# Index scores of a sparse-attention kernel: the low-key passes of two heads in the two halves of the array's rows

## The chip, the core and the metric

The kernel runs on one NeuronCore of a Trainium2 chip. The metric is the time on the device of one execution, in microseconds; lower is better.

## The reference, cut to what matters

The program is one step of a decoder layer: for a prompt of 2048 tokens and for 8 samples it computes a gated DeltaNet group and a sparse attention group from one input projection, then an output projection and a SwiGLU FFN. The change concerns the "lightning indexer" of the prompt's sparse attention, which scores every key for every query before the 256 best keys are chosen:

```python
def _index_scores(iq, ik, iw):
    dots = jnp.einsum('bqhd,bsd->bqhs', iq.astype(jnp.float32), ik.astype(jnp.float32))
    return jnp.einsum('bqh,bqhs->bqs', iw.astype(jnp.float32), jax.nn.relu(dots))
...
    def block(xs):
        q_b, iq_b, iw_b, t0 = xs
        qpos = t0 + jnp.arange(QBLOCK)
        score = _index_scores(iq_b, ik, iw_b)
        score = jnp.where(key_pos[None, None, :] <= qpos[None, :, None], score, -jnp.inf)
        _, idx = lax.top_k(score, topk)
```

There are 8 index heads of dimension 64, one key head for all of them, and blocks of 128 queries (16 blocks). Block i sees (i+1)·128 keys; blocks 0 and 1 need no scores, since they have no more than 256 keys.

## The kernel before, in words

**Split operands.** TensorE multiplies in a rounded format (float32r). So most operands are kept as a high part, rounded to that format, and a low part, the rest; `mm3` (L184 to L186) makes a projection or FFN product of three: high·high, high·low and low·high. These products, 128 × 128 by 512 columns, are the bulk of the work ("FFN products" below, though the input projection uses the same lines). They write PSUM banks tagged "d".

**The index.** A query head has 64 dimensions and the array 128 rows. So `tok` stores, per head, the high part in rows 0 to 63 and the low part in rows 64 to 127 of `iqT_d` (L1040 copies, L1041 subtracts, L1045 transposes), and `narrow` stores keys so that both halves of the rows hold the same high parts (tile a = 0) or the same low parts (a = 1). In `index`, per block and per chunk of up to 512 keys, each head makes two products over all 128 rows into one bank tagged "s" (L1721): (high + low query) with the high keys, then with the low keys. ScalarE applies relu from PSUM (L1723, tile `rl`), and VectorE multiplies by the head's weight and adds to the score row `sc` (L1726, L1728, L1730). There are two "s" banks, used by all of the side work: index, attention scores (L1766), transposes of the norm (L485) and others. `select` then finds the threshold of the 256 best, and `attend` does the attention: scores (L1766), transposed probabilities (L1795, "g" banks), values (L1783).

**Order.** PE runs in an order that a planner writes: `weave` keeps several generators (samples, indices, attends, and the feed, which is projection and FFN) and picks one at each step. A generator yields its PE time, a wait, and the bank that it needs next (`need`) or takes (`use`); `step` books when banks come free from planned times of VectorE and ScalarE. A share (`PACE`) sets when the feed goes ahead of the side work. Where the side work's planned PE time changes, the whole order behind it shifts. DMAs are issued by SP's queue in program order. The FFN of a group of 512 tokens (four groups, `ffn`) begins when the attention of its four blocks is done. Each FFN group has the output projection in 16 steps of 12 products, then a norm whose transposes (L485) need all of it, then the FFN's own steps.

**Other users of a part of the array.** The 32-wide inverse (L1079, L1087, L1092), its 64-wide step (L1122, L1127), the modulation in four strips of 32 columns (L424) and transposes of 8 rows for the samples (L2053) are products that use less than 128 rows or columns.

Of the kernel before, what the change touches and what calls it, by code (L numbers as in the profile page):

```python
# [25 lines left out]
F32 = mybir.dt.float32  # L26
F32R = mybir.dt.float32r
U8 = mybir.dt.uint8
BF = mybir.dt.bfloat16
AF = mybir.ActivationFunctionType  # L30
OP = mybir.AluOpType
# [81 lines left out]
class K:  # L113
# [442 lines left out]
    def weave(self, work, ends):  # L556

        ends = list(ends)
        while ends:
            for w in work:  # L560
                if w["until"] is not None and w["until"]():
                    w["at"], w["until"] = max(w["at"], self.now), None
            able = [(max(w["at"], min(self.free[w["need"]]) if w["need"] else 0), w) for w in work if w["until"] is None]
            self.now = max(self.now, min(t for t, w in able))
            able = [w for t, w in able if t <= self.now]
            w = next((w for w in able if w["early"] and self.spent >= self.share()), able[0])
            if w["early"]:
                with self.tc.high_priority(offset=EARLY):
                    said = next(w["run"], None)
            else:  # L570
                said = next(w["run"], None)
            if said is None:
                work.remove(w)
                if w in ends:
                    ends.remove(w)
            elif callable(said):
                w["until"], w["need"] = said, None
            else:
                self.step(w, *said[:2], **(said[2] if len(said) > 2 else {}))

    def step(self, w, pe, wait, use=None, hold=None, drop=None, need=None, after=False, by=None, **work):

        self.now += pe
        self.spent += 0 if w["early"] else pe
        ends = self.busy(w["early"], **work)
        end = (ends[by] if by else max(ends.values(), default=self.now - LAG)) + LAG
        for tag, at in ((use, end), (hold, GONE_BY)):
            if tag:
                f = self.free[tag]
                f[f.index(min(f))] = at  # L590
        if drop:
            f = self.free[drop]
            f[f.index(GONE_BY)] = end
        w["at"], w["need"] = max(self.now + wait, end if after else 0), need
# [381 lines left out]
    def tok(self, what, blk, a, rows):  # L976
        nc, p, O = self.nc, self.p1, self.O
        R = slice(0, rows)
        tk = slice(blk * 128, blk * 128 + 128)
        samp = blk == 16  # L980

        def P():
            return self.ps.tile([128, 512], F32, name="s", tag="s", bufs=2)

        if what == "aq":
            self.rope(a[R].rearrange("p (h d) -> p h d", h=H), self.ra, blk, rows, H, 16, "ropea")
            yield 0, 3
            pt = P()
            for h in range(H):
                self.o(nc.tensor.transpose(pt[:, h * rows:(h + 1) * rows], a[R, h * 128:(h + 1) * 128], self.id[R, R]))  # L990
            if samp:
                nc.scalar.copy(self.qTs, pt[:, :32].rearrange("p (h n) -> p h n", h=H))
                yield 0.1, 0
                return
            q = self.m("qo")[:, :512]
            nc.scalar.copy(q, pt)
            nc.sync.dma_start(self.qT_d[blk], q)
            yield TP, 0
        elif what == "kv":
            self.rope(a[R, 0:256].rearrange("p (h d) -> p h d", h=2), self.ra, blk, rows, 2, 16, "ropea")  # L1000
            yield 0, 2.5
            pt = P()
            for h in range(2):
                self.o(nc.tensor.transpose(pt[:, h * rows:(h + 1) * rows], a[R, h * 128:(h + 1) * 128], self.id[R, R]))
            pv = pt[:, :2 * rows].rearrange("p (h n) -> p h n", h=2)
            if samp:
                nc.scalar.copy(self.kTs, pv)
                nc.vector.tensor_copy(self.vs[R], a[R, 256:512])
                nc.sync.dma_start(O[7][0, :, 0].rearrange("n h d -> n (h d)"), a[R, 0:256])
                nc.sync.dma_start(O[8][0, :, 0].rearrange("n h d -> n (h d)"), a[R, 256:512])  # L1010
                yield 0.1, 0
                return
            q = self.m("qo")[:, :512]
            nc.scalar.copy(q[:, :256], pt[:, :256])
            nc.sync.dma_start(self.kT_d[:, :, tk].rearrange("h p n -> p h n"), q[:, :256].rearrange("p (h n) -> p h n", h=2))
            nc.sync.dma_start(self.V_d[tk], a[:, 256:512])
            nc.sync.dma_start(O[2][0, 0, tk].rearrange("n h d -> n (h d)"), a[:, 0:256])
            nc.sync.dma_start(O[3][0, 0, tk].rearrange("n h d -> n (h d)"), a[:, 256:512])
            yield TP / 2, 0
        else:  # L1020
            self.rope(a[R].rearrange("p (h d) -> p h d", h=8), self.ri, blk, rows, 8, 8, "ropei")
            if samp:
                yield 0, 3
                pt = P()
                for b in range(2):
                    x = self.m("iqs")[:NS, :512].rearrange("p (h a c) -> p h a c", h=4, a=2)
                    for e in range(2):
                        nc.scalar.copy(x[:, :, e, :], a[R, b * 256:(b + 1) * 256].rearrange("p (h c) -> p h c", h=4))
                    for h in range(4):
                        self.o(nc.tensor.transpose(pt[:, (b * 4 + h) * NS:(b * 4 + h + 1) * NS], x[:, h].rearrange("p a c -> p (a c)"), self.id[R, R]))  # L1030
                for e in range(2):
                    E = slice(e * 64, e * 64 + 64)
                    nc.scalar.copy(self.iqB[E, :, e * 8:e * 8 + 8], pt[E, :64].rearrange("p (h n a) -> p n a h", h=8, a=2)[:, :, e, :])
                yield 0.3, 0
                return

            for b in range(2):
                x = self.m("iqs", F32R)[:, :512].rearrange("p (h a c) -> p h a c", h=4, a=2)
                v = a[:, b * 256:(b + 1) * 256].rearrange("p (h c) -> p h c", h=4)
                nc.scalar.copy(x[:, :, 0, :], v)  # L1040
                nc.vector.tensor_tensor(x[:, :, 1, :], v, x[:, :, 0, :].bitcast(F32), op=OP.subtract)  # L1041
                yield 0, 2 if b else 5
                pt = P()
                for h in range(4):
                    self.o(nc.tensor.transpose(pt[:, h * 128:(h + 1) * 128], x[:, h].bitcast(F32).rearrange("p a c -> p (a c)"), self.id))  # L1045
                q = self.m("qo")[:, :512]
                nc.scalar.copy(q, pt)
                nc.sync.dma_start(self.iqT_d[blk, :, b * 512:(b + 1) * 512], q)
                yield TP, 0
# [657 lines left out]
    def index(self, i, B, general):  # L1707
        nc, p = self.nc, B["pool"]
        n = (i + 1) * 128
        if i >= 2:  # L1710
# [1 line left out]
            iq = B["iqT"]().rearrange("p (h n) -> p h n", h=8)  # L1712
            nc.sync.dma_start(iq, self.iqT_d[i].rearrange("p (h n) -> p h n", h=8))
            sc = B["sc"]()
            yield 0, 5, dict(need="s")
            for c, w in self.widths(n):
                s = sc[:, c * 512:c * 512 + w]
                for h in range(8):
                    ps = self.ps.tile([128, 512], F32, name="s", tag="s", bufs=2)
                    for a in range(2):  # L1720
                        self.o(nc.tensor.matmul(ps[:, :w], iq[:, h, :].bitcast(F32R), B["ikT"][c * 2 + a][:, :w].bitcast(F32R), start=a == 0, stop=a == 1))  # L1721
                    r = B["rl"]()
                    nc.scalar.activation(r[:, :w], ps[:, :w], AF.Relu)  # L1723
                    iw = self.iw[:, i, h:h + 1]
                    if h == 0:
                        nc.vector.tensor_scalar(s, r[:, :w], iw, None, op0=OP.mult)  # L1726
                    elif h == 7 and sums is not None:
                        nc.vector.scalar_tensor_tensor(s, r[:, :w], iw, s, op0=OP.mult, op1=OP.add, accum_out=sums[:, c:c + 1])  # L1728
                    else:
                        nc.vector.scalar_tensor_tensor(s, r[:, :w], iw, s, op0=OP.mult, op1=OP.add)  # L1730
                    yield 2 * MM * w / 512, max(0, self.load["dve"][1] - self.now - 0.8), dict(
                        act=0.16 + 0.44 * w / 512, dve=0.12 + 0.72 * w / 512, by="act", use="s", need="s")
            bias = B["bias"]()
            if general:
                nc.vector.tensor_tensor(sc[:, n - 128:n], sc[:, n - 128:n], self.caus, op=OP.add)
# [432 lines left out]
```

## Time and profile before

| | us |
|---|---|
| median of 3 runs (3600.11 to 3610.41) | 3608.34 |
| the profiled execution | 3607.71 |
| its span, first to last instruction | 3605.8 |
| PE busy in it | 3362.7 (93%) |
| index products, L1721, busy | 170.6 in two groups by tile: 576 and 32 |

Rows of the profile name line, engine, operation, output tile <- input tiles, then rows*columns of the array, the moving operand's shape, and the count. "Busy" of PE and the mean length of one product hold the pipeline's latency (about 0.4 us for a product that starts 0.23 us after the one before it); the time that a product takes from the others is the distance between starts, which the timeline shows. PEld rows are weight loads, which overlap products.

### The profile page before, as it was taken

To read this page: it belongs to the slowest core of one execution; us is meant where nothing else is said; L and a number is where in the kernel's file an instruction comes from. 1 tells how busy PE (TensorE), PEld (TensorE's weight loads), DVE (VectorE), ACT (ScalarE), POOL (GpSimd) and SP (SyncE) were. 2 spreads that over 40 slices of the span, in tenths; PEclk is the share of its full clock that TensorE was granted. 3 is DMA by queue.
4 is the path that set the end of the run, shared out by engine and by line. 5 is a ranking of instruction groups with operands and counts; after the bars stand their busy time and mean duration, and the time that the engine had idled before them with its cause. 6 is when DMAs were issued, how large, how long until landed. Compare 5 with 4: busy or idle time off the path is not lost.

```text
span 3605.8 us, 60166 instructions
## 1 busy us (share of the span) xinstructions
PE 3362.7 (93%) x21994; PEld 2601.9 (72%) x21994; DVE 2122.1 (59%) x4502; ACT 1472.4 (41%) x2855; POOL 593.4 (16%) x539
## 2 busy tenths in 40 slices
PE   8899989989997988999998999999899999899997
PEld 5667767767775767777766777777677777677775
DVE  5555635645743656666767655666766654554545
ACT  4333322422433333444456455454545643332323
POOL 1000001100000113222220121222112112222223
PEclk9999999999998999999999999999999999999999
DMA  8754764665686244455354344335433333522221
GB/s 287 241 185 157 224 232 145 219 221 175 212 274 212 92 143 126 140 165 164 122 200 140 119 148 152 102 105 194 138 95 108 98 102 103 181 76 82 78 83 57
DMA packets 421013, 549.60 MB, mean 152 GB/s; under 512 B 50020, under 2 KB 287817, under 8 KB 420698
## 3 DMA queue, kind: packets, MB, share of 16 engines
q1 hardware_dynamic: 420690, 545.62, 47.7%
q8 instruction: 175, 2.87, 0.3%
q14 instruction: 132, 1.08, 0.1%
q10 hardware_dynamic: 16, 0.03, 0.0%
HBM read 441.78 MB, written 122.70 MB: 157 GB/s over the span
## 4 chain that ended last, share of the span: by engine, by line
PE 53%; DVE 6%; issue 3%; ACT 2%; DMA 2%; SPq 1%; POOL 1%; DVEq 0%; ACTq 0%; POOLq 0%
PE d L184 13%; PE d L186 13%; PE d L185 12%; PE s L1721 3%; PE s L1766 3%; PE g L1783 3%; PE g L1795 1%; DVE wi L168 1%; PE g L200 1%; PE g L201 1%; DMA wr<-in_w_ffn_in_dram 1%; DMA wr<-in_w_out_dram 1%; ACT bias L1590 1%; ACT wi L167 0%; DVE ca L1857 0%
## 5 line engine op out<-in xcount | busy, mean ns | idle before, releaser
L184 PE MATMUL d<-hh,wi 128*128 128x512 f32 x1616 | 694.8, 430 | 26.5 <-DVE tm L1857 6.3
L185 PE MATMUL d<-hl,wi 128*128 128x512 f32 x1616 | 643.8, 398 | 5.3 <-DVE hl L489 5.1
L168 DVE TENSOR_TENSOR wi<-wr,wi 128x512 fp32r<-128x512 f32 x525 | 396.1, 755 | 419.6 <-ACT wi L167 413.9
L186 PE MATMUL d<-hh,wi 128*128 128x512 f32 x1616 | 643.0, 398 | 0.0
L167 ACT CAST wi<-wr 128x512 fp32r<-128x512 f32 x525 | 324.4, 619 | 702.4 <-PE d L186 396.4
L184 PEld LDWEIGHTS d<-hh,wi 128*128 128x128 f32 x1616 | 310.6, 192 | 122.4 <-issue 21.0
L185 PEld LDWEIGHTS d<-hl,wi 128*128 128x128 f32 x1616 | 311.2, 193 | 75.8 <-issue 10.1
L186 PEld LDWEIGHTS d<-hh,wi 128*128 128x128 f32 x1616 | 310.0, 192 | 69.8 <-DVE wi L168 0.4
L184 PE MATMUL d<-wi,hh 128*128 128x512 f32 x736 | 317.3, 431 | 19.1 <-DMA wi<-kept 11.5
L185 PE MATMUL d<-wi,hh 128*128 128x512 f32 x736 | 292.2, 397 | 0.4 <-DVE wi L168 0.4
L186 PE MATMUL d<-wi,hl 128*128 128x512 f32 x736 | 291.7, 396 | 0.3 <-issue 0.3
L184 PE MATMUL d<-wi,ah 128*128 128x512 f32 x616 | 263.4, 428 | 9.2 <-ACT ah L2102 5.4
L2103 POOL TENSOR_TENSOR al<-ca,ah 128x512 fp32r<-128x512 f32 x88 | 121.8, 1394 | 907.0 <-ACT ah L2102 906.8
L186 PE MATMUL d<-wi,al 128*128 128x512 f32 x616 | 245.2, 398 | 2.5 <-POOL al L2103 2.5
L185 PE MATMUL d<-wi,ah 128*128 128x512 f32 x616 | 244.2, 396 | 0.0
L1730 DVE SCALAR_TENSOR_TENSOR sc<-rl,iw,sc 128x512 f32<-128x512 f32 (+3 forms) x224 | 174.9, 781 | 75.0 <-ACT rl L1723 69.0
L1723 ACT ACTIVATE rl<-s 128x512 f32<-128x512 f32 (+3 forms) x288 | 151.4, 543 | 151.7 <-PE s L1721 127.5
L1858 POOL TENSOR_TENSOR xt<-xt,tm 128x512 f32<-128x512 f32 x96 | 141.2, 1482 | 401.3 <-DVE tm L1857 339.3
L184 PEld LDWEIGHTS d<-wi,hh 128*128 128x128 f32 x736 | 140.7, 191 | 64.1 <-DMA wi<-kept 16.2
L1590 ACT ACTIVATE bias<-sc,sv 128x640 bf16<-128x640 f32 (+11 forms) x120 | 169.9, 1416 | 35.7 <-DVE sv L1592 22.9
L1721 PE MATMUL s<-ik,iqT 128*128 128x512 f32 (+3 forms) x576 | 170.6, 392 | 9.2 <-DMA iqT<-iqT_d 4.9
L186 PEld LDWEIGHTS d<-wi,hl 128*128 128x128 f32 x736 | 140.5, 191 | 32.2 <-issue 0.3
(570 smaller groups left out, 5952.8 us busy)
## 6 DMA issues: line engine op xcount, KB each, us to landing
wi<-kept SPq DMA_DIRECT2D x168, 512.0 KB
wr<-in_w_ffn_in_dram SPq DMA_DIRECT2D x584, 128.0 KB
wr<-in_w_ffn_out_dram SPq DMA_DIRECT2D x148, 256.0 KB
kept<-wi SPq DMA_DIRECT2D x56, 512.0 KB
row<-in_w_ada_dram SPq DMA_DIRECT2D x32, 512.0 KB
wr<-in_w_in_dram SPq DMA_DIRECT2D x56, 256.0 KB
xt<-in_x_prompt_dram SPq DMA_DIRECT2D x7, 2048.0 KB
kT<-kT_d SPq DMA_DIRECT2D x54, 256.0 KB
```

What stands on the lines that cost most here:

```text
L167: nc.scalar.copy(hi, wr)
L168: nc.vector.tensor_tensor(lo, wr, hi.bitcast(F32), op=OP.subtract)
L184: self.o(nc.tensor.matmul(out, wh, xh, start=start, stop=False, **kw))
L185: self.o(nc.tensor.matmul(out, wh, xl, start=False, stop=False, **kw))
L186: self.o(nc.tensor.matmul(out, wl, xh, start=False, stop=stop, **kw))
L1590: nc.scalar.activation(c, s, AF.Sign, bias=t, accum_out=cnt)
L1721: self.o(nc.tensor.matmul(ps[:, :w], iq[:, h, :].bitcast(F32R), B["ikT"][c * 2 + a][:, :w].bitcast(F32R), start=a == 0, stop=a == 1))
L1723: nc.scalar.activation(r[:, :w], ps[:, :w], AF.Relu)
L1730: nc.vector.scalar_tensor_tensor(s, r[:, :w], iw, s, op0=OP.mult, op1=OP.add)
L1766: self.o(nc.tensor.matmul(ps[:, :w], qT[:, h, :], kT[:, :w], start=True, stop=True))
L1858: (nc.vector if soon else nc.gpsimd).tensor_tensor(xt, xt, tm, op=OP.add)
L2103: nc.gpsimd.tensor_tensor(al[b], a, ah[b].bitcast(F32), op=OP.subtract)
```

## The change

Heads are taken in pairs. Both heads make their product with the high keys over all 128 rows as before. The product with the low keys uses the high query part alone, over 64 rows: the even head's lies in rows 0 to 63, and odd heads are now stored the other way round, so that theirs lies in rows 64 to 127. The product of the two low parts is left out. The two 64-row products write different "s" banks. A pair now takes two banks at a time, and the planner learns to wait for two; it counts three products for a pair where it counted four.

```diff
-            able = [(max(w["at"], min(self.free[w["need"]]) if w["need"] else 0), w) for w in work if w["until"] is None]
+            able = [(max(w["at"], sorted(self.free[w["need"][0]])[len(w["need"]) - 1] if w["need"] else 0), w) for w in work if w["until"] is None]
...
-        for tag, at in ((use, end), (hold, GONE_BY)):
-            if tag:
+        for tags, at in ((use, end), (hold, GONE_BY)):
+            for tag in tags or ():
...
-                nc.scalar.copy(x[:, :, 0, :], v)
-                nc.vector.tensor_tensor(x[:, :, 1, :], v, x[:, :, 0, :].bitcast(F32), op=OP.subtract)
+                for e in range(2):
+                    nc.scalar.copy(x[:, e::2, e, :], v[:, e::2])
+                    nc.vector.tensor_tensor(x[:, e::2, 1 - e, :], v[:, e::2], x[:, e::2, e, :].bitcast(F32), op=OP.subtract)
...
-            yield 0, 5, dict(need="s")
+            yield 0, 5, dict(need="ss")
...
-                for h in range(8):
-                    ps = self.ps.tile([128, 512], F32, name="s", tag="s", bufs=2)
-                    for a in range(2):
-                        self.o(nc.tensor.matmul(ps[:, :w], iq[:, h, :].bitcast(F32R), B["ikT"][c * 2 + a][:, :w].bitcast(F32R), start=a == 0, stop=a == 1))
-                    r = B["rl"]()
-                    nc.scalar.activation(r[:, :w], ps[:, :w], AF.Relu)
...
-                    yield 2 * MM * w / 512, max(0, self.load["dve"][1] - self.now - 0.8), dict(
-                        act=0.16 + 0.44 * w / 512, dve=0.12 + 0.72 * w / 512, by="act", use="s", need="s")
+                for h2 in range(0, 8, 2):
+                    ps = [self.ps.tile([128, 512], F32, name="s", tag="s", bufs=2) for _ in range(2)]
+                    kh, kl = [B["ikT"][c * 2 + a][:, :w].bitcast(F32R) for a in range(2)]
+                    for e in range(2):
+                        self.o(nc.tensor.matmul(ps[e][:, :w], iq[:, h2 + e, :].bitcast(F32R), kh, start=True, stop=False))
+                    for e in range(2):
+                        half = slice(e * 64, e * 64 + 64)
+                        self.o(nc.tensor.matmul(ps[e][:, :w], iq[half, h2 + e, :].bitcast(F32R), kl[half], start=False, stop=True))
+                    for e in range(2):
+                        h = h2 + e
+                        r = B["rl"]()
+                        nc.scalar.activation(r[:, :w], ps[e][:, :w], AF.Relu)
...
+                    yield 3 * MM * w / 512, max(0, self.load["dve"][1] - self.now - 0.8), dict(
+                        act=0.32 + 0.88 * w / 512, dve=0.24 + 1.44 * w / 512, by="act", use="ss", need="ss")
```

What it does to the order is shown at three places. On PE, the first products of the index in the main loop over blocks (`ik_…` are the tiles of high and low keys, `iqT` the queries, `cf` the identity, `s` and `raws` the samples' convolution rows), before:

```order
L1333 MATMUL g<-cf,raws 8x128 x4
L1721 MATMUL s<-ik_14209,iqT 128x512
L1721 MATMUL s<-ik_14210,iqT 128x512
L184 MATMUL d<-hh,wi 128x512
L185 MATMUL d<-hl,wi 128x512
L186 MATMUL d<-hh,wi 128x512
```

and after:

```order
L1334 MATMUL g<-cf,raws 8x128 x4
L1723 MATMUL s<-ik_14306,iqT 128x512 x2
L1726 MATMUL s<-ik_14307,iqT 128x512 x2
L184 MATMUL d<-hh,wi 128x512
L185 MATMUL d<-hl,wi 128x512
L186 MATMUL d<-hh,wi 128x512
```

One head's two products have become one pair's four, the last two of 64 rows (L1726). Between pairs stand three FFN products or more.

On PE at the norm in the third FFN group (`xt` the rows to transpose, `big` and `PT` the attention's probabilities, `hh`, `hl` the normalised rows), before:

```order
L186 MATMUL d<-wi,hl 128x512
L1795 MATMUL g<-cf,big 128x128 x8
L1783 MATMUL g<-PT,V 128x256 x2
L1795 MATMUL g<-cf,big 128x128 x4
L1783 MATMUL g<-PT,V 128x256 x2
L485 MATMUL s<-cf,xt 128x128 x8
L1795 MATMUL g<-cf,big 128x128 x4
L1783 MATMUL g<-PT,V 128x256 x2
L184 MATMUL d<-hh,wi 128x512
```

and after (L1773 is the line of the attention's scores):

```order
L186 MATMUL d<-wi,hl 128x512
L485 MATMUL s<-cf,xt 128x128 x8
L1773 MATMUL s<-kT,qT 128x512
L184 MATMUL d<-hh,wi 128x512
L185 MATMUL d<-hl,wi 128x512
```

Sixteen transposes and six value products of attention have left this place, and one score product has come. At the same place of the second group 17 products other than the norm's stood before, and 34 now. The last attention block ends 183 FFN products ahead of the fourth group before, and 45 now.

On ScalarE, in a block of the index with a chunk of 512 and one of 384 keys (`rl<-s` are the relus, `PT<-g` the attention's copies, `wi<-wr` the weights' casts), before:

```order
L1723 ACTIVATE rl<-s 128x512 x2
L167 CAST wi<-wr 128x512
L1798 COPY PT<-g 128x512
L1723 ACTIVATE rl<-s 128x512 x2
L1798 COPY PT<-g 128x512
L1723 ACTIVATE rl<-s 128x512 x2
```

and after:

```order
L1730 ACTIVATE rl<-s 128x512 x2
L1805 COPY PT<-g 128x512
L167 CAST wi<-wr 128x512
L1730 ACTIVATE rl<-s 128x512 x2
L1805 COPY PT<-g 128x512 x2
L1730 ACTIVATE rl<-s 128x512 x2
```

The relus come in twos there in both; what stands between two twos has moved by a copy or a cast.

More of the change, by code (lines that the diff above doesn't have):

```diff
@@ L1714, in index @@
             sc = B["sc"]()
-            yield 0, 5, dict(need="s")
+            yield 0, 5, dict(need="ss")
             for c, w in self.widths(n):
                 s = sc[:, c * 512:c * 512 + w]
-                for h in range(8):
-                    ps = self.ps.tile([128, 512], F32, name="s", tag="s", bufs=2)
-                    for a in range(2):
-                        self.o(nc.tensor.matmul(ps[:, :w], iq[:, h, :].bitcast(F32R), B["ikT"][c * 2 + a][:, :w].bitcast(F32R), start=a == 0, stop=a == 1))
-                    r = B["rl"]()
[L1723 to L1730, printed above, removed]
-                    yield 2 * MM * w / 512, max(0, self.load["dve"][1] - self.now - 0.8), dict(
-                        act=0.16 + 0.44 * w / 512, dve=0.12 + 0.72 * w / 512, by="act", use="s", need="s")
@@ new lines, in index @@
+                for h2 in range(0, 8, 2):
[10 more added lines that the diff above has]
+                        nc.scalar.activation(r[:, :w], ps[e][:, :w], AF.Relu)
+                        iw = self.iw[:, i, h:h + 1]
+                        if h == 0:
+                            nc.vector.tensor_scalar(s, r[:, :w], iw, None, op0=OP.mult)
+                        elif h == 7 and sums is not None:
+                            nc.vector.scalar_tensor_tensor(s, r[:, :w], iw, s, op0=OP.mult, op1=OP.add, accum_out=sums[:, c:c + 1])
+                        else:
+                            nc.vector.scalar_tensor_tensor(s, r[:, :w], iw, s, op0=OP.mult, op1=OP.add)
+                    yield 3 * MM * w / 512, max(0, self.load["dve"][1] - self.now - 0.8), dict(
+                        act=0.32 + 0.88 * w / 512, dve=0.24 + 1.44 * w / 512, by="act", use="ss", need="ss")
```

## The prediction

> **What bounds the kernel now.** I read the page's busy shares first, then its chain of work that ended last, then the table of windows for the stretch in which the index runs.
>
> ```profile
> PE 3362.7 (93%) x21994; PEld 2601.9 (72%) x21994; DVE 2122.1 (59%) x4502; ACT 1472.4 (41%) x2855; POOL 593.4 (16%) x539
> ...
> PE 53%; DVE 6%; issue 3%; ACT 2%; DMA 2%; SPq 1%; POOL 1%; DVEq 0%; ACTq 0%; POOLq 0%
> ```
> ```profile
> core 0: us, PE busy (x) PEld busy (x) DVE busy (x) ACT busy (x) POOL busy (x), PEclk, DMA share, GB/s
> 944.00:2853.00 1909.00, 1788.64 (x9810) 1387.39 (x9808) 1202.10 (x2553) 901.45 (x1658) 344.75 (x302) 0.97 0.47 146
> ```
> TensorE is busy 93% of the span and holds most of the chain. In the 1909 us from the first index product to the last it is busy 94% at a granted clock of 0.97; VectorE has 63% and ScalarE 47%. PE runs its instructions in written order, and projection or FFN products stand between nearly all index products. So a microsecond added to or taken from PE there is, but for little, a microsecond of the span.
>
> **What the removed products cost.** The rows by form give the number of index products of each width, two per head, so four per pair of heads.
>
> ```profile
> L1721 PE MATMUL s<-ik,iqT 128*128 128x512 f32 x432 | 140.8, 420 | 8.6 <-DMA iqT<-iqT_d 4.9 <-ACT rl L1723 3.6
> ...
> L1721 PE MATMUL s<-ik,iqT 128*128 128x384 f32 x48 | 12.4, 352 | 0.1
> ...
> L1721 PE MATMUL s<-ik,iqT 128*128 128x256 f32 x48 | 9.0, 289 | 0.5 <-ACT rl L1723 0.5
> ...
> L1721 PE MATMUL s<-ik,iqT 128*128 128x128 f32 x48 | 8.4, 274 | 0.0
> ...
> L1721 PE MATMUL s<-gzc,sq 128*128 128x512 f32 x16 | 4.9, 399 | 0.0
> ...
> L1721 PE MATMUL s<-gzc,sq 128*128 128x384 f32 x16 | 4.2, 352 | 0.9 <-ACT decb L1723 0.9
> ```
> (432+16)/4 = 112 pairs of width 512, (48+16)/4 = 16 of 384, 12 of 256 and 12 of 128: 152 pairs, or 112 + 16·0.75 + 12·0.5 + 12·0.25 = 133 in units of 512 columns. The means (420 ns) hold the pipeline's latency and are no price. The price is the distance between starts, in the timeline of one head among FFN products (start, length, engine and line):
>
> ```profile
> 2818.06 0.39 PE L186 MATMUL d<-hh,wi 128*128 128x512 f32 x1
> 2818.29 0.62 PE L1721 MATMUL s<-ik,iqT 128*128 128x512 f32 x2
> 2818.75 0.39 PE L184 MATMUL d<-hh,wi 128*128 128x512 f32 x1
> ```
> Two products take 2818.75 − 2818.29 = 0.46 us, 0.23 each, and weight loads are hidden. A pair's two second passes are thus 0.46 us at 512 columns; I scale the others by width. If the two halves run side by side they take one stream of 0.23, and the other 0.23 is the gain: 133 × 0.23 = 30.6 us.
>
> **What the new form adds: leaving and re-entering the whole array.** No product of 64 rows and 128 columns is in this trace, so I bound its cost by the products that use a part of the array. The row nearest in shape is the transposes at L2053: 8 rows, all 128 weight columns, alone between FFN products.
>
> ```profile
> 3579.69 0.40 PE L186 MATMUL d<-kT,al 128*128 128x512 f32 x1
> 3580.01 0.28 PE L2053 MATMUL s<-cf,s 8*128 8x8 f32 x2
> 3580.23 0.50 PE L184 MATMUL d<-wi,ah 128*128 128x512 f32 x1
> 3580.56 0.39 PE L185 MATMUL d<-wi,ah 128*128 128x512 f32 x1
> ```
> ```profile
> 3580.01 0.19 PEld L2053 LDWEIGHTS s<-cf,s 8*128 8x128 f32 x2 [0.37 <-issue]
> 3580.22 0.19 PEld L184 LDWEIGHTS d<-wi,ah 128*128 128x128 f32 x1
> 3580.33 0.19 PEld L185 LDWEIGHTS d<-wi,ah 128*128 128x128 f32 x1
> ```
> The start after L186 comes 0.32 later, not 0.23, and the weight load starts only then, after 0.37 us of idling in which nothing is waited for: it isn't pulled ahead. On the way back the load of L184 starts with the product itself, and the product after it comes 0.33 later. From L186 to L185 pass 0.87 us; the two whole products in it are 0.46; so two loads of 128 columns with nearly nothing streamed (8 columns) cost 0.41 us. In the new kernel's pair two loads of 128 columns stand in the same place, with a stream behind them. Two other excursions bound this.
>
> ```profile
> 237.81 0.40 PE L186 MATMUL d<-wi,hl 128*128 128x512 f32 x1
> 238.14 1.14 PE L1122 MATMUL g<-low,NT 64*64 64x64 f32 x16
> 239.21 0.50 PE L184 MATMUL d<-wi,hh 128*128 128x512 f32 x1
> 239.55 0.39 PE L185 MATMUL d<-wi,hh 128*128 128x512 f32 x1
> ```
> ```profile
> 448.81 0.39 PE L186 MATMUL d<-wi,hl 128*128 128x512 f32 x1
> 449.12 1.06 PE L424 MATMUL s<-row,cT 128*32 128x512 f32 x8
> 450.12 0.50 PE L184 MATMUL d<-wi,hh 128*128 128x512 f32 x1
> 450.46 0.39 PE L185 MATMUL d<-wi,hh 128*128 128x512 f32 x1
> ...
> L424 PE MATMUL s<-row,cT x128: 592/617/1062, 449.1 to 1150.5; 128*32 128x512 f32 x128
> ```
> The 64x64 products start one every (1.14 − 0.22)/15 = 0.06 us by an estimate that takes 0.22 for the last one's own length (as the 0.28 of L2053's two suggests); of 239.55 − 237.81 − 0.46 = 1.28 us the 16 of them take 0.98, which leaves 0.30 for the way there and back with loads of 64 columns. L424 shows the other thing: eight products in four column strips, none shorter than 0.592 us, fit into 1.06 us, so strips do run side by side; L424's way there and back also shows 0.31 to the first start and 0.34 after L184. So the fixed price is 0.30 to 0.41 us a pair; I take 0.41, since the loads are of 128 columns as in L2053.
>
> The sum on PE is 152 × 0.41 − 30.6 = 62.3 − 30.6 = +31.7 us; at 0.30 it would be 45.6 − 30.6 = +15. At 512 columns a pair loses 0.41 − 0.23 = 0.18 us, at 128 columns 0.35: no width gains.
>
> The Trainium skill (TensorEngine Tiling (Array Packing), Key Properties) says that changing the tiling mode drains TensorE; the 0.32 instead of 0.23 after L186 agrees. The page gives no price for the drain, so by its rule alone the sum could not be made.
>
> **The other parts.** The pair needs both banks of "s" free, a head needed one.
>
> ```profile
>   ACT rl L1723: 14.4, 23
> ...
> L1723 ACT ACTIVATE rl<-s 128x512 f32<-128x512 f32 x216 | 125.0, 596 | 115.8 <-PE s L1721 94.7 <-DMA V<-V_d 11.8 <-DVE sc L1730 5.0
> ```
> Index products and their weight loads waited 14.4 us for the relu, in 23 places. A pair holds both banks for two relus, 2 × 0.60 = 1.2 us, behind whatever cast or copy ScalarE has just begun (0.6 each). In the new order three FFN products (0.69 us) are the least that stands between close pairs, mostly with eight transposes and value products of the attention, or with nine FFN products. What would be queued behind a waiting product is PE's whole stream. The bounds are −10 (most of today's waits go, since fewer places can wait) and +15 (a tenth of a microsecond at each of 152 pairs); I take +2.
>
> Storing odd heads the other way round makes two ScalarE copies and two VectorE subtractions of each one:
>
> ```profile
> L1041 DVE TENSOR_TENSOR iqs<-tk,iqs 128x256 fp32r<-128x256 f32 x32 | 13.5, 422 | 12.8 <-ACT iqs L1040 11.4 <-issue 0.9
> L1040 ACT CAST iqs<-tk 128x256 fp32r<-128x256 f32 x32 | 13.0, 407 | 0.2
> ```
> At no more than 0.41 us for each half, that is at most 32 × 0.41 = 13 us more on each of two engines that idle half of the time: nothing on PE, unless the transposes of L1045 come sooner than their input; they stand behind a planned pause of 5 us (2 for the second half), so I book 0.
>
> The written order moves attention work. At the norm between the two halves of the third FFN group, 16 transposes and six value products of attention filled part of a PE gap, and now one score product does.
>
> ```profile
> 2556.72 0.40 PE L186 MATMUL d<-wi,hl 128*128 128x512 f32 x1
> 2556.96 1.03 PE L1795 MATMUL g<-cf,big 128*128 128x128 f32 x8
> 2559.27 1.13 PE L1783 MATMUL g<-PT,V 128*128 128x256 f32 x4 [1.28 <-ACT PT L1798]
> ...
> 2572.80 0.99 PE L184 MATMUL d<-hh,wi 128*128 128x512 f32 x1
> ```
> The gap of 16 us is the norm's; 22 products' worth, some 4 us, must now be paid elsewhere, while the same place one group earlier gets about as many more than it had. I take 0 for the two, within ±4. The last attention block also ends closer to the fourth FFN group, which waits for it: before, that group started without a pause.
>
> ```profile
> 3084.58 0.40 PE L186 MATMUL d<-wi,al 128*128 128x512 f32 x1
> 3084.82 0.40 PE L184 MATMUL d<-wi,hh 128*128 128x512 f32 x1
> ...
> 3074.70 0.36 SPq L1926 DMA_DIRECT2D hl<-oTl_d  x1
> ```
> Its last input was asked for 10 us ahead on SP's queue and is used only in the seventh and eighth of its steps (2.8 us each); 45 FFN products, 10 us, are still left between in the new order. What is late next is that load, and the weight loads queued behind it on SP; cost 0, at most 5.
>
> The sum is 31.7 + 2 = about +33 on the profiled execution's 3607.7 us (span 3605.8), which lies 0.6 under the median of 3608.3; I round to 3640. A difference under 0.3% (11 us) is about what a measurement of this kernel can't tell from no change.
>
> **The rivals.** First, faster: the halves need no way there and back. Then a pair costs one stream less and no more: −30.6, 3577 us. For it speaks that L424's strips overlap; against it that each of the excursions shown starts 0.09 late and pays again on its way back. It decides at a price of 30.6/152 = 0.20 us a pair: below that the change gains. The Trainium skill (TensorE: Matmul & The Clock Gate, Part 3) gives this outcome if its span model is taken alone: packed products take one product's time and some 4 ns for each further tile. The trace agrees on the overlap but its 0.41 us is not in that model.
>
> Second, slower still: halves that share the 128 columns don't run side by side. L424's strips have columns of their own, so nothing here shows row halves sharing them. Then the gain of 30.6 falls away: +62.3, 3672 us. In between, the second half's weight load may line up behind the first: L184 and L185's loads start 3580.33 − 3580.22 = 0.11 apart where L2053's two came closer, so at most another 152 × 0.11 = 17 us, 3657.
>
> Third, the order hides it: the excursions fall where PE would have waited anyway. PE idles 1909 − 1789 = 120 us in the stretch; if a quarter of the pairs' cost met it and the lower price held, +15 × 0.75 and the −10 of the bank waits leave about 0, 3609 us. Against it: FFN products stand right behind nearly every pair.
>
> **How the numbers follow.** The likeliest case, a fixed price of 0.3 to 0.45 us with overlapped halves, gets 0.62; its own range is 3608 + 15 to 3608 + 48, the upper end being the sum with +15 of bank waits. Halves or loads in line get 0.15, the free switch 0.10, the hidden one 0.13. So faster is 0.11 (the free switch and a little of the third), same 0.13, slower 0.76. The range from 3613 to 3668 holds the first case, loads in line and part of the third.
>
> **What would show it.** Right: second passes as 64*128 products whose two starts lie within 0.02 us; 0.32 us from the last whole product to their weight load; 0.33 us between the next FFN product and the one after it; about 1.1 us from the first whole product of a pair to the FFN product behind it; PE's busy share hardly changed. Wrong: a start 0.23 after the whole product (free switch), starts 0.2 apart (no overlap), or new waits of the index for the relu of over 20 us.

## The result, and the profile after

The changed kernel took 3641.76 us (median of 4 runs, 3640.64 to 3645.03) against 3609.2 for the kernel before on the same chip: 32.6 us more, a ratio of 1.0098 with a 95% interval of 1.0082 to 1.0114 (30 to 41 us). Its profiled span is 3639.9 us. First the page of the changed kernel, shares of busy time and the chain:

```profile
PE 3379.0 (93%) x21994; PEld 2565.6 (70%) x21994; DVE 2129.5 (59%) x4534; ACT 1469.7 (40%) x2887; POOL 582.8 (16%) x539
...
PE 59%; DVE 8%; DMA 7%; issue 4%; ACT 3%; SPq 2%; POOL 0%; ACTq 0%; DVEq 0%; POOLq 0%
```

PE has as many instructions as before and the same share, and the granted clock is the same (0.971 before, 0.972 now). PE is busy 16 us more, and idle 3639.9 − 3379.0 = 261 us instead of 3605.8 − 3362.7 = 243, 18 us more. The timeline of one pair among FFN products (PE, then its weight loads) shows what a pair has become:

```profile
1801.41 0.39 PE L186 MATMUL d<-hh,wi 128*128 128x512 f32 x1
1801.64 0.63 PE L1723 MATMUL s<-ik,iqT 128*128 128x512 f32 x2
1802.19 0.50 PE L1726 MATMUL s<-ik,iqT 64*128 64x512 f32 x2
1802.62 0.50 PE L184 MATMUL d<-hh,wi 128*128 128x512 f32 x1
1802.96 0.39 PE L185 MATMUL d<-hl,wi 128*128 128x512 f32 x1
```
```profile
1802.19 0.19 PEld L1726 LDWEIGHTS s<-ik,iqT 64*128 64x128 f32 x2 [0.36 <-issue]
1802.62 0.19 PEld L184 LDWEIGHTS d<-hh,wi 128*128 128x128 f32 x1 [0.24 <-issue]
```

The two 64-row products fill one record of 0.50 us together, and so do their loads (0.19 for both): they run side by side. But their loads start only after 0.36 us in which no weight load runs, and L184's load again starts only with its own product, 0.43 us later. From L186 to L185 pass 1802.96 − 1801.41 = 1.55 us; without the two whole FFN products (0.46) the pair costs 1.09 us. Four whole products cost 4 × 0.23 = 0.92. The pair shown is like the others: of the 39 pairs of 512 columns that stand between FFN products, the median from L186 to L185 is 1.55 us. The view of the second passes' line shows what the gap ahead of them is put down to:

```profile
L1726 PE MATMUL s<-ik,iqT x288: 323/496/792, 1345.7 to 2940.5; 64*128 64x512 f32 x108, 64*128 64x128 f32 x12, 64*128 64x256 f32 x12, 64*128 64x384 f32 x12
...
its engine sat idle before it (us, times) until:
  issue: 43.7, 126
```

"Issue" is time in which the engine waited for nothing that the profile shows: no operand is late. That the array is being emptied in it is a reading; the runs below show what a trip costs, not what happens inside it.

### The profile page after: what moved, and what is told of

The parts are those of the page before. It is cut to its first block, busy times and chain, and to the rows that moved or that the text cites. A ratio compares the mean times of both kernels' runs of the same rounds, so it can differ in the third digit from the quotient of the medians.

```text
span 3639.9 us, 60287 instructions
## 1 busy us (share of the span) xinstructions
PE 3379.0 (93%) x21994; PEld 2565.6 (70%) x21994; DVE 2129.5 (59%) x4534; ACT 1469.7 (40%) x2887; POOL 582.8 (16%) x539
## 3 DMA queue, kind: packets, MB, share of 16 engines
q14 instruction: 133, 1.09, 0.1%
## 4 chain that ended last, share of the span: by engine, by line
PE 59%; DVE 8%; DMA 7%; issue 4%; ACT 3%; SPq 2%; POOL 0%; ACTq 0%; DVEq 0%; POOLq 0%
PE d L184 14%; PE d L185 13%; PE d L186 13%; PE g L1790 3%; PE s L1773 3%; PE g L1802 2%; PE s L1723 2%; PE s L1726 2%; DVE wi L168 1%; DMA wr<-in_w_ffn_in_dram 1%; DMA wi<-kept 1%; PE g L200 1%; PE g L201 1%; DMA wr<-in_w_out_dram 1%; ACT bias L1591 1%
## 5 line engine op out<-in xcount | busy, mean ns | idle before, releaser
L184 PE MATMUL d<-hh,wi 128*128 128x512 f32 x1616 | 696.8, 431 | 29.3 <-DVE th L2104 9.3
L185 PE MATMUL d<-hl,wi 128*128 128x512 f32 x1616 | 643.9, 398 | 1.5 <-DVE hl L489 1.3
L186 PE MATMUL d<-hh,wi 128*128 128x512 f32 x1616 | 642.6, 398 | 0.0
L184 PEld LDWEIGHTS d<-hh,wi 128*128 128x128 f32 x1616 | 310.7, 192 | 131.0 <-issue 25.7
L186 PEld LDWEIGHTS d<-hh,wi 128*128 128x128 f32 x1616 | 310.1, 192 | 69.6 <-DVE wi L168 0.4
L185 PEld LDWEIGHTS d<-hl,wi 128*128 128x128 f32 x1616 | 311.3, 193 | 67.5 <-issue 7.9
L184 PE MATMUL d<-wi,hh 128*128 128x512 f32 x736 | 313.9, 427 | 26.3 <-DMA wi<-kept 10.0
L185 PE MATMUL d<-wi,hh 128*128 128x512 f32 x736 | 292.8, 398 | 7.8 <-DVE wi L168 7.6
L186 PE MATMUL d<-wi,hl 128*128 128x512 f32 x736 | 291.8, 396 | 0.3 <-issue 0.3
L184 PE MATMUL d<-wi,ah 128*128 128x512 f32 x616 | 269.1, 437 | 14.5 <-DVE th L2104 6.5
L186 PE MATMUL d<-wi,al 128*128 128x512 f32 x616 | 244.8, 397 | 2.1 <-POOL al L2110 2.1
L185 PE MATMUL d<-wi,ah 128*128 128x512 f32 x616 | 243.8, 396 | 0.0
L184 PEld LDWEIGHTS d<-wi,hh 128*128 128x128 f32 x736 | 140.5, 191 | 76.8 <-DMA wi<-kept 14.6
L1730 ACT ACTIVATE rl<-s 128x512 f32<-128x512 f32 (+3 forms) x288 | 141.3, 540 | 130.7 <-PE s L1726 121.5
L185 PEld LDWEIGHTS d<-wi,hh 128*128 128x128 f32 x736 | 141.1, 192 | 35.2 <-DVE wi L168 10.1
L186 PEld LDWEIGHTS d<-wi,hl 128*128 128x128 f32 x736 | 140.6, 191 | 31.3
```

Source lines behind the costliest of these rows:

```text
L184: self.o(nc.tensor.matmul(out, wh, xh, start=start, stop=False, **kw))
L185: self.o(nc.tensor.matmul(out, wh, xl, start=False, stop=False, **kw))
L186: self.o(nc.tensor.matmul(out, wl, xh, start=False, stop=stop, **kw))
L1730: nc.scalar.activation(r[:, :w], ps[e][:, :w], AF.Relu)
```

## The experiments

The rivals were, for the loss: a fixed price of each trip to 64-row products and back (A), or the pairs' two banks and the order that they move (B); and for the halves, that they overlap or that they don't (C). All ratios are to the kernel before on the same chip; the first four variants ran together, and so did the last four. The changed kernel ran with neither, so a step from it to a variant is the difference of two ratios, good to some 8 to 12 us.

**Whole second passes, same pairs and order.** PE's order of the main program is that of the changed kernel, product for product.

```diff
-                        self.o(nc.tensor.matmul(ps[e][:, :w], iq[half, h2 + e, :].bitcast(F32R), kl[half], start=False, stop=True))
+                        self.o(nc.tensor.matmul(ps[e][:, :w], iq[:, h2 + e, :].bitcast(F32R), kl, start=False, stop=True))
```

> The changed kernel with its pairs, its two banks and its order, but both second passes over all 128 rows again (all four products, as in the kernel before). Theory A (each trip to 64-row products and back costs a fixed 0.39 us a pair, 152 pairs, 59 us, against one stream of about 30 us saved): the trips are gone, so the time falls back to 3609 plus what the moved order costs, 3604 to 3620. Rival B (the pairs' two banks and the moved order cost the time, and the halves gain their 30 us as meant): the loss stays and the gain goes, about 3672.

Measured: ratio 1.0038 (1.0025 to 1.0052), 14 us over the kernel before. The timeline of a pair:

```profile
2697.39 0.39 PE L186 MATMUL d<-hh,wi 128*128 128x512 f32 x1
2697.62 0.62 PE L1723 MATMUL s<-ik,iqT 128*128 128x512 f32 x2
2698.07 0.62 PE L1725 MATMUL s<-ik,iqT 128*128 128x512 f32 x2
2698.53 0.39 PE L184 MATMUL d<-hh,wi 128*128 128x512 f32 x1
```

The pair takes 2698.53 − 2697.62 = 0.91 us. So B falls as it was put, with its 3672: with everything but the trips and the saved stream in place the loss is 14 us, and the step to the changed kernel, 1.0098 − 1.0038 = 0.60% or 22 us (the two intervals allow some 8 either way), is the trips less the stream saved. But the 14 us were more than expected.

**Both 64-row products in the same half.** Odd heads are stored like even ones again, as in the kernel before, and the slice changes:

```diff
-                        half = slice(e * 64, e * 64 + 64)
+                        half = slice(0, 64)
```

> The changed kernel, but all heads stored alike, so that both 64-row products of a pair use rows 0 to 63, one after the other. Theory A says the halves overlap in the changed kernel, so here a pair costs one stream more, 133 times 0.23 = 31 us, and perhaps an uncovered weight load of 0.1 at each of 152 pairs: 3672 to 3690. Rival C (the halves never overlapped): no change, 3642.

Measured: 1.0156 (1.0127 to 1.0185), 0.58% or 21 us over the changed kernel.

```profile
2158.87 0.39 PE L186 MATMUL d<-hh,wi 128*128 128x512 f32 x1
2159.10 0.62 PE L1722 MATMUL s<-ik,iqT 128*128 128x512 f32 x2
2159.65 0.73 PE L1725 MATMUL s<-ik,iqT 64*128 64x512 f32 x2
2160.31 0.50 PE L184 MATMUL d<-hh,wi 128*128 128x512 f32 x1
2160.64 0.39 PE L185 MATMUL d<-hl,wi 128*128 128x512 f32 x1
```
```profile
2159.65 0.29 PEld L1725 LDWEIGHTS s<-ik,iqT 64*128 64x128 f32 x2 [0.36 <-issue]
```

The pair now costs 2160.64 − 2158.87 − 0.46 = 1.31 us, 0.22 more than 1.09: one whole stream. C falls: the halves of the changed kernel overlap fully. The second load in the same half is hidden too (both loads are over in 0.29 us, while the first product still streams), so there was no further 0.1 a pair. The time rose by less than the 3672 to 3690 expected (30 to 48 us over the changed kernel).

**Twice the trips.** Chunks of 512 keys in two column halves; the columns streamed are the same.

```diff
+                    for q in ([slice(0, w)] if w < 512 else [slice(0, 256), slice(256, 512)]):
...
+                            self.o(nc.tensor.matmul(ps[e][:, q], iq[half, h2 + e, :].bitcast(F32R), kl[half, q], start=False, stop=True))
```

> The changed kernel, but in chunks of 512 keys each pair is worked in two column halves of 256: two whole products, two 64-row products, and again. The columns streamed stay the same, the trips double in 112 pairs. Theory A: 112 times 0.39 = 44 us more, 3675 to 3695. Rival B: within 10 us of 3642, since order, banks and relus are the same.

Measured: 1.0220 (1.0197 to 1.0242), 1.22% or 44 us over the changed kernel, as A had it.

```profile
2173.61 0.39 PE L186 MATMUL d<-hh,wi 128*128 128x512 f32 x1
2173.83 0.40 PE L1724 MATMUL s<-ik,iqT 128*128 128x256 f32 x2
2174.16 0.38 PE L1727 MATMUL s<-ik,iqT 64*128 64x256 f32 x2
2174.47 0.50 PE L1724 MATMUL s<-ik,iqT 128*128 128x256 f32 x2
2174.90 0.39 PE L1727 MATMUL s<-ik,iqT 64*128 64x256 f32 x2
2175.22 0.50 PE L184 MATMUL d<-hh,wi 128*128 128x512 f32 x1
2175.55 0.40 PE L185 MATMUL d<-hl,wi 128*128 128x512 f32 x1
```

The pair costs 2175.55 − 2173.61 − 0.46 = 1.48 us, 0.39 more than with one trip; 112 × 0.39 = 44.

**No second passes.** The two lines of the 64-row products are dropped.

> The changed kernel without the second passes (the products with the low keys are left out). Theory A: both the trips (59 us) and the one stream left (30 us) go, 3642 - 89 = 3553, or 61 us under the variant with whole second passes; 3540 to 3565. Rival B: only the one stream goes, about 3611.

Measured: 0.9908 (0.9887 to 0.9928), 33 us under the kernel before and 1.90% or 69 us under the changed one. By the starts (1.09 − 0.46 at 512 columns, and less at the narrow widths) PE got about 90 us of work less. So A's direction and most of its size are there and B's 3611 is not, but some quarter of the PE time did not come out as time: PE's idle time is 3571.7 − 3296.0 = 276 us here, 15 more than in the changed kernel.

**Trips with next to no stream.** All but 8 of their columns are cut.

```diff
-                        self.o(nc.tensor.matmul(ps[e][:, :w], iq[half, h2 + e, :].bitcast(F32R), kl[half], start=False, stop=True))
+                        self.o(nc.tensor.matmul(ps[e][:, :8], iq[half, h2 + e, :].bitcast(F32R), kl[half, :8], start=False, stop=True))
```

> The changed kernel with its 64-row products cut to 8 columns (the rest of the products with the low keys is left out): the trips stay, their stream goes. On PE a pair of 512 should take 1.09 - 0.21 = 0.88 us from its neighbours' starts. Theory A (the trip has a fixed price of 0.4 us, whatever is streamed): about 28 us of PE time fewer than the changed kernel and 59 more than the variant without second passes. Since the first four variants moved the time by some 0.7 to 0.8 of the PE time that their pairs lost or gained, 0.55 to 0.8% under the changed kernel, 3612 to 3622 where the kernel before takes 3606, and 1.1 to 1.5% above the variant without second passes. A rival in which the price grows with the stream: close to that variant, under 3590.

Measured: 1.0011 (0.9995 to 1.0026), 0.87% or 31 us under the changed kernel, and 1.03% or 37 us above the variant without second passes, a little under the 1.1 to 1.5% expected. So of the 152 × 0.39 = 59 us of PE time by which it differs from that variant, some two thirds show as time.

```profile
1557.92 0.39 PE L186 MATMUL d<-wi,al 128*128 128x512 f32 x1
1558.14 0.62 PE L1723 MATMUL s<-ik,iqT 128*128 128x512 f32 x2
1558.69 0.27 PE L1726 MATMUL s<-ik,iqT 64*128 64x8 f32 x2
1558.90 0.49 PE L184 MATMUL d<-wi,ah 128*128 128x512 f32 x1
1559.23 0.39 PE L185 MATMUL d<-wi,ah 128*128 128x512 f32 x1
```

The pair costs 1559.23 − 1557.92 − 0.46 = 0.85 us, 0.39 more than the two whole products alone (0.46). That is the trip by itself, at 8 columns as at 256. The 31 us against the changed kernel agree with the one stream that the latter still pays (133 × 0.23).

**Where the 14 us come from.** Three variants: the other storing alone in the kernel before, whole second passes with a planner that counts four products for a pair, and the kernel before, head by head, with the planner's share of the side work at 440 for 463.

> The kernel before, with only the other storing of odd heads (two copies and two subtractions in place of one; both 128-row products of a head still sum over both halves, so nothing else changes). If the 14 us that pairs with whole products cost were the storing's, this shows them: +8 to +14. If they are the order's, within 4 us of the kernel before.

Measured: 1.0003 (0.9986 to 1.0021). No cost of the storing shows; the interval leaves at most 8 us.

```diff
-                    yield 3 * MM * w / 512, max(0, self.load["dve"][1] - self.now - 0.8), dict(
+                    yield 4 * MM * w / 512, max(0, self.load["dve"][1] - self.now - 0.8), dict(
```

> The variant of pairs with whole second passes, but the planner counts four products for a pair, as it did for two heads before, where it counted three. If the wrong count moved the order to its cost, the time comes back to the kernel before, 0 to +5 us. If taking heads by twos does it (two relus and two multiply-adds at a time, two banks at a time), it stays at +8 to +18.

Measured: 1.0029 (1.0015 to 1.0044), 10 us; not told apart from the count of three.

```diff
-MM, TP, F4, LAG, EARLY, PACE, GONE_BY = 0.23, 0.46, 0.88, 0.6, 3000, 463, 1e9
+MM, TP, F4, LAG, EARLY, PACE, GONE_BY = 0.23, 0.46, 0.88, 0.6, 3000, 440, 1e9
```

> The kernel before with one number of the planner changed (the share of the side work 440 for 463), heads one by one as before: the last attention block then ends about as late among the FFN products as in the changed kernel. If it is the later place of the attention that costs, +8 to +14 us; if it is the pairs, within 5 us of the kernel before. It also shows how far a mere moving of the order shifts the time.

Measured: 1.0053 (1.0034 to 1.0072), 19 us. So moving the order can cost as much without any pair as with pairs. It is another order than that of the pairs, though: its last attention block ends right at the fourth group's start, where 45 FFN products stand between in the changed kernel. PE's waits, of the kernel before and of the pairs with whole products (line waited, releaser, us, times, longest), name who is late:

```profile
PE d L184 <- DVE tm L1857: 9.8, 11, 3.7
...
PE s L1721 <- ACT rl L1723: 4.1, 7, 0.9
...
PE d L184 <- DVE th L2097: 3.8, 5, 1.6
...
PE d L184 <- DVE ca L2099: 2.8, 4, 1.9
...
PE d L184 <- DVE ca L1857: 2.5, 4, 0.9
...
PE s L1766 <- ACT rl L1723: 1.6, 3, 1.1
...
PE d L185 <- DVE wi L168: 0.4, 1, 0.4
```
```profile
PE d L184 <- DVE th L2103: 17.6, 12, 3.0
...
PE d L184 <- ACT wi L167: 8.7, 7, 4.5
...
PE d L184 <- DVE ca L1863: 7.5, 8, 1.6
...
PE d L184 <- DVE ca L2105: 7.2, 6, 2.3
...
PE d L185 <- DVE wi L168: 6.4, 6, 3.8
...
PE d L184 <- DVE tm L1863: 1.6, 4, 0.8
```

FFN products wait for VectorE to empty "d" banks (tm, th and ca, which it computes from them, together: 19 us became 34) and for the casts of their weights (wi: 0.4 became 15). PE's idle time in all rose by less, from 243 to 3613.8 − 3351.1 = 263 us, since other waits fell. In the kernel before with another share the first kind grew as well, to 29 us, and the second did not:

```profile
PE d L184 <- DVE ca L2099: 11.1, 10, 2.3
PE d L184 <- DVE tm L1857: 9.0, 10, 3.4
...
PE d L184 <- DVE th L2097: 7.2, 6, 2.7
...
PE d L184 <- DVE ca L1857: 1.8, 3, 1.1
...
PE d L185 <- DVE wi L168: 0.5, 1, 0.5
```

What is open: whether twos of relus and multiply-adds add anything of their own to this. The waits for casts speak for it: with pairs, the profiles have some 12 us or more of them (13.8 in the changed kernel), and without pairs 2 us at most. But every order with pairs also puts the attention later, so no run here separates the two. Plans that book the pairs sooner were not run.

## Why the prediction was right

3640 was forecast and 3641.76 measured, and the mechanism is the one named. That the sum came within 2 us is luck: one term was too high and another too low by about as much.

- **Way there and back.** Forecast: start 0.32 after the last whole product, 0.33 on the way back, halves side by side, about 1.1 us a pair. Measured: 0.32 (two whole products at 1801.64 and 0.23 later, load at 1802.19), 0.34, one record for both, 1.09. The transposes of 8 rows had shown 0.41 for the trip; it is 0.39. By starts, the change costs PE (1.09 − 0.92) × 112 at 512 columns and about 9 at the narrow widths, some 28 us, where the sum had 31.7. Scaling by width missed at 128 columns: in the trace of whole second passes such products start 0.11 us apart, not 0.06, so a pair loses 0.18 us there and not 0.35. In time that cost, against the variant with whole second passes, is 22 give or take 8.
- **A microsecond of PE is one of the span.** Right within the intervals for some steps (twice the trips: 44 of 44, give or take 10; streams cut to 8 columns: 31 of some 30), too simple for others: without the second passes 69 of 90 us came out, and the step from there to the bare trips, up again, shows 37 of 59, give or take 9.
- **The order.** This is the term that was mis-sized: +2 ± some 10 for bank waits, norm gaps and the end of the attention together, and 14 (9 to 19) measured. The bank waits got the +2. The index's own went down (its products and weight loads waited 14.4 us before and 4.4 now; the 14.4 held idle time of the weight loads, of PE's it was 4.1). But others that use the "s" banks wait for the relu instead, and PE's waits for it rose from 5.7 to 10.6 us in all. The norm gap of the third group and the fourth group's start hold next to no loss: that gap shrank from 16.1 to 13.5 us when attention work left it, and the fourth group starts after a pause of 0.36.

```profile
  ACT rl L1730: 4.4, 5
...
PE s L1773 <- ACT rl L1730: 4.2, 6, 0.7
...
PE s L485 <- ACT rl L1730: 2.9, 5, 0.7
...
PE s L1468 <- ACT rl L1730: 1.8, 1, 1.8
...
PE s L1723 <- ACT rl L1730: 1.7, 1, 1.7
...
2533.82 0.39 PE L186 MATMUL d<-wi,hl 128*128 128x512 f32 x1
...
2547.30 1.42 PE L184 MATMUL d<-hh,wi 128*128 128x512 f32 x1
...
3115.91 0.47 PE L184 MATMUL d<-wi,hh 128*128 128x512 f32 x1 [0.36 <-ACT wi L167]
```

  What the forecast did not look at is the FFN's own VectorE and ScalarE work, which stands in the same two queues as the index's; the waits above show that it came later in many small places. The trips' term was some 4 us (by starts) to 10 us (by time) too high and the order's 12 too low.
- **The storing.** Booked at 0; its ratio is 1.0003 ± 0.0018.
- **The rivals.** The free switch needed a trip under 0.20 us; it is 0.39. Halves that share columns and don't overlap were worth 62 us; the variant with one half shows that they do overlap. The order that hides the trips did not: it added. The prediction read L424's overlap from lengths, which hold the latency and prove none; the overlap holds all the same, since eight streams of 0.23 would be 1.84 us and they fit into 1.06.

The Trainium skill (TensorEngine Tiling (Array Packing), Key Properties) has the drain at a change of tiling mode; the trace agrees in the late start after it (0.32 us, not 0.23) and adds the price of the trip here, 0.39 us there and back. Its span model for packed products (TensorE: Matmul & The Clock Gate, Part 3) gives a pair of halves one stream and a few ns; the trace agrees (both in one record, and 0.22 us more when they share a half), and the model leaves the trip's price out.

None of the variants that keep the products with the low keys beats the kernel before; the one that is faster leaves them out. A trip would have to carry more than 0.39/0.23 = 1.7 streams saved, so two pairs at a time would gain 2 × 0.23 − 0.39 = 0.07 us at 512 columns, an estimate from these prices, less than 76 × 0.07 = 5 us in all, and would need four banks where the order of two already cost 14 us.

## What to carry to other kernels

Two half-height products side by side save one stream, but a short trip to such products and back between whole ones has a price: here 0.39 us, whatever was streamed, 1.7 products of 512 columns. Look for any small product in the trace that already makes such a trip, take its distance between whole products, and multiply by the number of trips before counting streams; by this price packing pays only where one trip saves two streams or more. And in a kernel whose order is planned by hand, price a moved order by a control that moves it without the change: here 10 to 20 us, a third to a half of what the change cost.

## What the runs showed that was not expected

- The trip's price does not depend on what is in it: 0.39 with 8 columns, 0.39 for the second trip with 256, and within one half a second load and product cost only their stream, 0.22.
- A microsecond of PE time was worth between about two thirds of one and a whole one of the span: 37 of 59 and 69 of 90 us, but 44 of 44 for the second trips. Why the steps differ is open.
- The index's second bank is paid by others: its own waits for the relu fell, and those of the attention scores and the norm's transposes rose.
